# Layer 1's gate and up products by seven block products, in two phases of 512 tokens

## The chip, the cores and the metric

The kernel runs on one core of a Trainium2 chip. The metric is the device time of one execution in microseconds (us). The core has TensorE (PE in the profile; its weight loads are listed as PEld), VectorE (DVE), ScalarE (ACT), GpSimd (POOL) and SyncE (SP), which issues most DMAs. The engines run their own instruction streams in order and meet at semaphores.

## The reference

A block of two layers works on 1024 latent tokens of width 1024, with 256 context tokens as a prefix. Layer 0 mixes Fourier groups with windowed attention, layer 1 is a two-dimensional neighbourhood attention on a grid of 16 rows by 64 columns. Each layer ends in a SwiGLU FFN of width 2816:

```
def _swiglu(h, wg, wu, wd):
    return (jax.nn.silu(h @ wg) * (h @ wu)) @ wd
...
        x = x + g1 * o
        h = _rms(x, norm2_g[i]) * (1.0 + sc2) + sh2
        x = x + g2 * _swiglu(h, ffn_w_gate[i], ffn_w_up[i], ffn_w_down[i])
```

In the last layer only the latent tokens are kept. The case concerns layer 1 from its output projection (o before `x + g1 * o`) to the end.

## The kernel before

Everything stands transposed: 128 channels on the partitions, tokens along the free axis. A width of 1024 is eight tiles (KT = 8), 2816 is 22 tiles (NF = 22). Each fp32 number is split in two fp32r parts, hi (a rounded copy) and lo (the rest), and each product of tiles is three matmuls, hi by hi, hi by lo, lo by hi (`mm3`, L72 to L76, the three PE lines of the profile). So weights and activations both have to be split: a CAST on ACT gives hi, a subtraction on DVE gives lo.

In layer 1, `Dense` (L740 on) does the output projection, the norm, and the FFN. `weights` (L769 to L777) loads a raw tile of 128x1024 on the SP queue into one of two raw slots, casts it on ACT (L775), subtracts on DVE (L776), into a ring of four hi/lo tiles. `out_proj` (L779) makes each of eight output tiles over 24 matmuls of 512 columns into PSUM (`d_ps`), and DVE adds it to the residual x (L793). It runs twice, for tokens 0 to 511 and 512 to 1023; beside the second run go the norm of the first half (`norm`, L799 to L834: squares on ACT, sums on POOL or DVE, then nrm_t, h_hi, h_lo).

`ffn` (L836) walks over the 22 f tiles. `gate_up` makes, for each f and each half of the tokens, gate (`g_ps`) and up (`u_ps`), 24 matmuls of 512 columns each, then Silu on ACT (L860), the product on DVE (L862) and its split (L863 on ACT, L864 on DVE). `down` takes a block of two or three f's, and makes for each half eight chunks `d_ps` of 6 or 9 matmuls, which DVE adds to x (L878). Both halves use the same split weights: a weight is loaded and split once. x is kept in row order, and attention's output is in the order of grid columns, so x is read and written through a rearranged view (`xs`, `by_col`). In the last block each finished tile of x leaves as one DMA of 512 KB on ACT's queue (L1225).

Attention before it (L1087 to L1211) has its order written out by hand; its last matmuls are `po` (L1168), whose splits (L1177) write the tiles h_hi and h_lo (L1071). Elsewhere in this stage, the build's scheduler sets each engine's order, from the order of the code and its own estimate of when operands are there, and each engine then keeps to it. A tile pool with n buffers lets a new tile wait until an old one's last reader is done.

## Time and profile before

| | us |
|---|---|
| median of 3 runs (lowest, highest) | 2942.49 (2939.51, 2943.05) |
| the profiled execution | 2940.7 |
| its span, first to last instruction | 2938.9 |
| PE busy in it | 2860.1 |
| DVE, ACT, POOL busy in it | 1381.5, 875.5, 313.6 |
| first `d_ps` of layer 1's output projection starts at | 2095.0 |

The page first gives busy times by engine, then 40 equal slices with the clock granted to TensorE, the DMA queues, the chain of work that ended last, the costliest groups of instructions, and the DMAs. Groups are written `line engine operation out<-in shape xcount | busy us, mean ns of one | idle of the engine before them, and what ended it`. A timeline row starts with the start and the duration in us, and `[3.23 <-PE ...]` behind it is the idle time before it and what ended that. A PE row's duration includes the pipeline, so the pace of matmuls is read from the distance of their starts.

### The profile page before, as it was taken

To read this page: it belongs to the slowest core of one execution; us is meant where nothing else is said; L and a number is where in the kernel's file an instruction comes from. 1 tells how busy PE (TensorE), PEld (TensorE's weight loads), DVE (VectorE), ACT (ScalarE), POOL (GpSimd) and SP (SyncE) were. 2 spreads that over 40 slices of the span, in tenths; PEclk is the share of its full clock that TensorE was granted. 3 is DMA by queue.
4 is the path that set the end of the run, shared out by engine and by line. 5 is a ranking of instruction groups with operands and counts; after the bars stand their busy time and mean duration, and the time that the engine had idled before them with its cause. 6 is when DMAs were issued, how large, how long until landed. Compare 5 with 4: busy or idle time off the path is not lost. (4 is left out here: it accounts for less than half of the span.)

```text
span 2938.9 us, 38168 instructions
## 1 busy us (share of the span) xinstructions
PE 2860.1 (97%) x15290; PEld 2316.5 (79%) x15290; DVE 1381.5 (47%) x2530; ACT 875.5 (30%) x1672; POOL 313.6 (11%) x442
## 2 busy tenths in 40 slices
...
PEclk9989999999999999999999999999999999999999
...
GB/s 277 75 128 222 214 218 151 65 43 36 29 51 29 44 29 44 44 36 37 44 81 149 107 109 153 180 180 161 130 79 44 50 51 43 43 51 51 43 48 67
DMA packets 117218, 267.20 MB, mean 91 GB/s; under 512 B 9232, under 2 KB 67088, under 8 KB 110000
## 3 DMA queue, kind: packets, MB, share of 16 engines
...
## 5 line engine op out<-in xcount | busy, mean ns | idle before, releaser
L775 ACT CAST w_hi<-w_raw 128x1024 fp32r<-128x1024 f32 x188 | 195.3, 1049 | 881.3 <-PE d_ps L75 488.4
L878 DVE SCALAR_TENSOR_TENSOR x<-d_ps,mod,x 128x512 f32<-128x512 f32 (+1 forms) x400 | 348.1, 880 | 166.4 <-PE d_ps L76 165.9
L776 DVE TENSOR_TENSOR w_lo<-w_raw,w_hi 128x1024 fp32r<-128x1024 f32 x184 | 224.2, 1226 | 287.9 <-ACT w_hi L775 283.3
L862 DVE TENSOR_TENSOR sg<-sg,u_ps 128x512 f32<-128x512 f32 (+1 forms) x110 | 69.8, 634 | 570.5 <-PE u_ps L76 570.5
L74 PE MATMUL d_ps<-act_hi,w_hi 128*128 128x512 f32 (+1 forms) x880 | 328.0, 373 | 3.4 <-DVE x L878 3.4
L75 PE MATMUL d_ps<-act_lo,w_hi 128*128 128x512 f32 (+1 forms) x880 | 327.9, 373 | 1.3 <-DVE act_lo L864 1.3
L76 PE MATMUL d_ps<-act_hi,w_lo 128*128 128x512 f32 (+1 forms) x880 | 328.0, 373 | 0.0
L74 PEld LDWEIGHTS d_ps<-act_hi,w_hi 128*128 128x128 f32 x880 | 165.7, 188 | 37.4 <-DVE x L878 5.6
L75 PEld LDWEIGHTS d_ps<-act_lo,w_hi 128*128 128x128 f32 x880 | 165.7, 188 | 32.5 <-DVE act_lo L864 1.7
L76 PEld LDWEIGHTS d_ps<-act_hi,w_lo 128*128 128x128 f32 x880 | 165.7, 188 | 31.2
L75 PE MATMUL u_ps<-o_lo,w_hi 128*128 128x512 f32 (+1 forms) x528 | 188.6, 357 | 0.0
L76 PE MATMUL u_ps<-o_hi,w_lo 128*128 128x512 f32 (+1 forms) x528 | 188.6, 357 | 0.0
L74 PE MATMUL u_ps<-o_hi,w_hi 128*128 128x512 f32 (+1 forms) x528 | 188.6, 357 | 0.0
L76 PE MATMUL g_ps<-o_hi,w_lo 128*128 128x512 f32 (+1 forms) x528 | 188.5, 357 | 0.0
L75 PE MATMUL g_ps<-o_lo,w_hi 128*128 128x512 f32 (+1 forms) x528 | 188.5, 357 | 0.0
L74 PE MATMUL g_ps<-o_hi,w_hi 128*128 128x512 f32 (+1 forms) x528 | 188.5, 357 | 0.0
L580 POOL TENSOR_SCALAR pr<-pr,st 128x640 f32<-128x640 f32 (+2 forms) x208 | 156.0, 751 | 266.6 <-DVE st L579 176.0
L574 ACT ACTIVATE pr<-sm,st 128x640 f32<-128x640 f32 (+4 forms) x208 | 162.7, 782 | 31.1 <-POOL sm L563 22.3
L810 POOL TENSOR_TENSOR nrm_ss<-nrm_ss,nrm_sq 128x512 f32<-128x512 f32 (+1 forms) x38 | 48.4, 1274 | 1058.5 <-PE d_ps L76 935.6
L863 ACT CAST act_hi<-sg 128x512 fp32r<-128x512 f32 (+1 forms) x110 | 63.6, 578 | 298.3 <-DVE sg L862 298.3
L589 PE MATMUL pt_ps<-ident,pr 128*128 128x128 f32 x944 | 139.0, 279 | 5.8 <-ACT pt L593 2.8
L75 PE MATMUL g_ps<-h_lo,w_hi 128*128 128x512 f32 x352 | 139.6, 397 | 1.0 <-DVE h_lo L829 1.0
...
## 6 DMA issues: line engine op xcount, KB each, us to landing
...
w_raw<-w_gate SPq DMA_DIRECT2D x44, 512.0 KB, 3.2
w_raw<-w_up SPq DMA_DIRECT2D x44, 512.0 KB, 3.2
w_raw<-w_down SPq DMA_DIRECT2D x44, 512.0 KB, 3.2
...
w_raw<-w_out SPq DMA_DIRECT2D x32, 512.0 KB, 3.3
w_raw<-w_in SPq DMA_DIRECT2D x24, 512.0 KB, 4.4
q<-q_d SPq DMA_DIRECT2D x14, 512.0 KB, 16.8
```

The costliest lines, as they stand in the source:

```text
L74: TE.matmul(out, lh, rh, start=first, stop=False)
L75: TE.matmul(out, lh, rl, start=False, stop=False)
L76: TE.matmul(out, ll, rh, start=False, stop=last)
L574: S.activation(self.pr[:, :n], self.sm[:, :n], AF.Exp, bias=st[:, 0:1], scale=-1.0, accum_out=st[:, 1:2])
L580: G.tensor_scalar(self.pr[:, :n], self.pr[:, :n], st[:, 3:4], 0.0, ALU.mult, ALU.add)
L589: TE.transpose(pt[:, b * P:(b + 1) * P], self.pr[:, (b0 + b) * P:(b0 + b + 1) * P], ident)
L775: S.copy(hi, raw)
L776: eng.tensor_tensor(lo, raw, fl(hi), ALU.subtract)
L810: adder(i).tensor_tensor(ss, ss, sq, ALU.add)
L862: V.tensor_tensor(sg[:, :n], sg[:, :n], u_ps[:, :n], ALU.mult)
L863: S.copy(a_hi[:, sl], sg[:, :n])
L878: V.scalar_tensor_tensor(xs, self.shaped(ps[:, :n]), vec(l, 5)[:, dt, v:v + 1], xs, ALU.mult, ALU.add)
```

## The change

For one f, gate and up together are a product of a 2x2 block matrix of weights with a 2x2 block matrix of activations: the two halves of the 1024 input channels (k = 0 to 3, and 4 to 7) by gate and up, and two halves of 256 tokens. The new code computes it with seven block products instead of eight, by a scheme of Strassen's kind. It needs four sums of activation blocks (`combine`, made once per phase on POOL, then split by ACT and DVE to `c_hi`, `c_lo`) and four differences of weight blocks per f (`t1` to `t4`, on POOL). `gate_up1` has for each f and phase 7 products of 4 tiles by 3 matmuls of 256 columns, ACT casts of the seven weight blocks of 128x512, the lo parts of five on DVE and of two (b21, b22) on POOL, and additions of the products on DVE out of PSUM. The FFN runs once for tokens 0 to 511 and once for 512 to 1023, so each raw weight is loaded and split twice.

The output projection is also rewritten in two phases (`out_proj1`): x is now kept in grid-column order, the old residual is loaded again for each tile (`x_old`), and weights are split in halves of 128x512 into a ring of six. Raw weights, `x_old`, the block sums `s_sum` and later `h_in` share four slots of 128x1024. The normalized activations of the second phase are kept in DRAM (`h_d`) and loaded at the phase boundary. The down weights are split into the room of the attention output (`w_room`, named h1_hi and h1_lo in the rows below), two sets used in turn. The output leaves in eight DMAs of 256 KB per phase in column order, and the host's rearrangement of the result follows it.

```diff
-    bg, bg_cm = pools.open("big1", side="right")
-    h_hi = bg.tile([P, KT, SEQ], F32R, name="h_hi")
-    h_lo = bg.tile([P, KT, SEQ], F32R, name="h_lo")
+
+    h_out, bg_cms = [None, None], [None, None]
+    for i in (1, 0):
+        bg, bg_cms[i] = pools.open(f"big1{i}", side="right")
+        h_out[i] = [bg.tile([P, KT, 512], F32R, name=f"h{i}_{n}") for n in ("hi", "lo")]
...
-            hi, lo = (h[:, pr, g * 256:(g + 1) * 256] for h in (h_hi, h_lo))
+            hi, lo = (h[:, pr, g % 2 * 256:(g % 2 + 1) * 256] for h in h_out[g // 2])
...
-    dl = Dense(1, SEQ, (C0, C1), h_hi, h_lo, x, by_col=True)
-    own = norm2(C0)
-    dl.out_proj(io["w_out1"], (C0,), lambda dt: nc.sync.dma_start(x[:, dt], x_d[:, dt]), (own,))
-    last = norm2(C1, lambda i: V)
-    dl.out_proj(io["w_out1"], (C1,), None, (last,), own)
...
+    wr, wr_cm = pools.open("raw1", bufs=4)
+    ww, ww_cm = pools.open("ring1", bufs=6)
+    wk, wk_cm = pools.open("wk1")
+    pd, pd_cm = pools.open("pd1", bufs=2, psum=True)
+    pm, pm_cm = pools.open("pm1", bufs=1, psum=True)
+    pp, pp_cm = pools.open("pp1", bufs=5, psum=True)
+    HT = 256
+
+    def raw_weights(src):
+        raw = wr.tile([P, KT, P], F32, name="w_raw")
+        nc.sync.dma_start(raw, src)
+        return raw
+
+    def parts_of(src, eng=V):
+
+        hi, lo = (ww.tile([P, 4, P], F32R, name=n) for n in ("w_hi", "w_lo"))
+        S.copy(hi, src)
+        eng.tensor_tensor(lo, src, fl(hi), ALU.subtract)
+        return hi, lo
+
+    def out_proj1(ci, own, side=iter(())):
+        h_hi, h_lo = h_out[ci]
+        for dt in reversed(range(KT)):
+            raw = raw_weights(io["w_out1"][dt])
+            ws = [parts_of(raw[:, i:i + 4]) for i in (0, 4)]
+            old = wr.tile([P, SEQ], F32, name="x_old", tag="w_raw")
+            nc.sync.dma_start(old, x_d[:, dt])
+            ps = pd.tile([P, 512], F32, name="d_ps")
+            for k in range(KT):
+                hi, lo = ws[k // 4]
+                mm3(ps, hi[:, k % 4], lo[:, k % 4], h_hi[:, k], h_lo[:, k], k == 0, k == KT - 1)
+            cols = slice(ci * 32, ci * 32 + 32)
+            V.scalar_tensor_tensor(x[:, dt, ci * 512:ci * 512 + 512].rearrange("p (c r) -> p c r", r=GH),
+                                   ps.rearrange("p (c r) -> p c r", r=GH), vec(1, 2)[:, dt, 0:1],
+                                   old.rearrange("p (r c) -> p c r", c=GW)[:, cols], ALU.mult, ALU.add)
+            advance(own, 1)
+            advance(side, 3)
...
+    def norm1s(ci, adder, done):
...
+            both = []
+            for k in (i, i + 4):
+                t = wk.tile([P, 512], F32, name="nrm_t", tag="t", bufs=4)
+                V.scalar_tensor_tensor(t, x[:, k, ts], nA[3][:, k, 0:1], r, ALU.mult, ALU.mult)
+                h = wk.tile([P, 512], F32, name="nrm_h", bufs=2)
+                S.activation(h, t, AF.Identity, bias=vec(1, 3)[:, k, 0:1], scale=1.0)
+                both.append(h)
+                yield
+            done(i, *both)
...
+    def combine(i, h0, h4):
+        s = wr.tile([P, 4, HT], F32, name="s_sum", tag="w_raw")
+        G.tensor_tensor(s[:, 0], h0[:, M2], h4[:, M2], ALU.add)
+        G.tensor_tensor(s[:, 1], s[:, 0], h0[:, M1], ALU.subtract)
+        G.tensor_tensor(s[:, 2], h0[:, M1], h0[:, M2], ALU.subtract)
+        G.tensor_tensor(s[:, 3], h4[:, M1], s[:, 1], ALU.subtract)
+        for sl, src in ((slice(0, 1), h0[:, M1].unsqueeze(1)),
+                        (slice(1, 3), h4.rearrange("p (a n) -> p a n", a=2)), (slice(3, 7), s)):
+            S.copy(c_hi[:, sl, i], src)
+            V.tensor_tensor(c_lo[:, sl, i], src, fl(c_hi[:, sl, i]), ALU.subtract)
+
+    def product7(w, slot):
+        ps = pp.tile([P, 512], F32, name="p_ps")[:, 0:HT]
+        for k in range(4):
+            mm3(ps, w[0][:, k], w[1][:, k], c_hi[:, slot, k], c_lo[:, slot, k], k == 0, k == 3)
+        return ps
...
+    def gate_up1(f, side=iter(())):
+        g, u = raw_weights(io["w_gate"][1, f]), raw_weights(io["w_up"][1, f])
+        b11, b21, b12, b22 = g[:, 0:4], g[:, 4:8], u[:, 0:4], u[:, 4:8]
+        t1, t2, t3, t4 = (wk.tile([P, 4, P], F32, name=n, tag="t", bufs=4) for n in ("t1", "t2", "t3", "t4"))
+        p1, u2, u3, sg = (wk.tile([P, HT], F32, name=n) for n in ("p1", "u2", "u3", "sg"))
+        av = wk.tile([P, 2, HT], F32, name="av", bufs=2)
+        hi, lo = (wk.tile([P, 512], F32R, name=n, bufs=4) for n in ("act_hi", "act_lo"))
+        w = parts_of(b11)
+        G.tensor_tensor(t1, b12, b11, ALU.subtract)
+        G.tensor_tensor(t2, b22, t1, ALU.subtract)
+        ps = product7(w, 0)
+        S.copy(p1, ps)
+        w = parts_of(t2)
+        G.tensor_tensor(t3, b22, b12, ALU.subtract)
+        ps = product7(w, 4)
+        V.tensor_tensor(u2, ps, p1, ALU.add)
+        w = parts_of(t3)
+        G.tensor_tensor(t4, t2, b21, ALU.subtract)
+        ps = product7(w, 5)
+        V.tensor_tensor(u3, ps, u2, ALU.add)
+        w = parts_of(t1)
+        ps = product7(w, 3)
+        V.tensor_tensor(av[:, 1], ps, u3, ALU.add)
+        V.tensor_tensor(u2, ps, u2, ALU.add)
+        w = parts_of(t4)
+        ps = product7(w, 2)
+        V.tensor_tensor(u3, u3, ps, ALU.subtract)
+        S.activation(u3, u3, AF.Silu)
+        w = parts_of(b21, G)
+        ps = product7(w, 1)
+        V.tensor_tensor(av[:, 1], av[:, 1], u3, ALU.mult)
+        V.tensor_tensor(sg, ps, p1, ALU.add)
+        S.activation(sg, sg, AF.Silu)
+        w = parts_of(b22, G)
+        ps = product7(w, 6)
+        V.tensor_tensor(u2, ps, u2, ALU.add)
+        V.tensor_tensor(av[:, 0], u2, sg, ALU.mult)
+        avf = av.rearrange("p a n -> p (a n)")
+        S.copy(hi, avf)
+        V.tensor_tensor(lo, avf, fl(hi), ALU.subtract)
+        advance(side, 6)
+        return hi, lo
...
+    w_room = [t.rearrange("p k n -> p (k n)").rearrange("p (f h t k n) -> p f h t k n", f=2, h=2, t=2, n=P)
+              for t in h_out[1]]
...
+    def down1(ci, fs, acts, last):
+        w_in = w_room[fs[0] // 2 % 2]
+        ts = slice(ci * 512, ci * 512 + 512)
+        raws = [raw_weights(io["w_down"][1, f]) for f in fs]
+        for h in range(2):
+            for i, raw in enumerate(raws):
+                src = raw[:, 4 * h:4 * h + 4]
+                S.copy(w_in[:, i, h, 0], src)
+                V.tensor_tensor(w_in[:, i, h, 1], src, fl(w_in[:, i, h, 0]), ALU.subtract)
+            for dt in range(4 * h, 4 * h + 4):
+                ps = pd.tile([P, 512], F32, name="d_ps")
+                for i in range(2):
+                    mm3(ps, w_in[:, i, h, 0, dt % 4], w_in[:, i, h, 1, dt % 4], *acts[i], i == 0, i == 1)
+                V.scalar_tensor_tensor(x[:, dt, ts], ps, vec(1, 5)[:, dt, 0:1], x[:, dt, ts], ALU.mult, ALU.add)
+                if last:
+                    nc.scalar.dma_start(io["out"][:, dt, ts], x[:, dt, ts])
...
+    own0 = norm1s(0, G, combine)
+    out_proj1(0, own0)
...
+    own1 = norm1s(1, V, keep)
+    out_proj1(1, own1, own0)
+    advance(own0, 99)
+    for ci in range(2):
+        acts = {}
+        for f in range(NF):
+            acts[f] = gate_up1(f, own1)
+            if f % 2 == 0 and 2 <= f < NF - 2:
+                down1(ci, (f - 2, f - 1), [acts.pop(f - 2), acts.pop(f - 1)], False)
+        for f in (NF - 4, NF - 2):
+            down1(ci, (f, f + 1), [acts.pop(f), acts.pop(f + 1)], f == NF - 2)
+            if f == NF - 4 and ci == 0:
+                for i in range(4):
+                    h = wr.tile([P, 2, 512], F32, name="h_in", tag="w_raw")
+                    for n in range(2):
+                        nc.sync.dma_start(h[:, n], h_d[:, i + 4 * n])
+                    combine(i, h[:, 0], h[:, 1])
...
-    return np.ascontiguousarray(o.transpose(2, 1, 0).reshape(1, SEQ, D))
+
+    o = o.reshape(P, KT, GW, GH).transpose(3, 2, 1, 0)
+    return np.ascontiguousarray(o.reshape(1, SEQ, D))
```

Three places of the order. Rows are: line, operation, output<-inputs, shape; the number behind a name tells tiles apart.

First, DVE at the start of the second output projection. Before (x(18372) and x(18423) are the adds of its first and second tile, w_lo 18464 and 18499 the weights of its third and fourth):

```order
L776 TENSOR_TENSOR w_lo_18464<-w_raw_18461,w_hi_18463 128x1024
L793 SCALAR_TENSOR_TENSOR x_18001<-d_ps_18313,mod1_72,x_18001 128x32x16
L776 TENSOR_TENSOR w_lo_18499<-w_raw_18496,w_hi_18498 128x1024
L82 TENSOR_TENSOR nrm_v_18344<-nrm_v_18344 128x4
L83 SCALAR_TENSOR_TENSOR nrm_v_18344<-nrm_v_18344 128x4
L84 SCALAR_TENSOR_TENSOR nrm_v_18344<-nrm_v_18344 128x4
L827 SCALAR_TENSOR_TENSOR nrm_t_18357<-x_18001,nA3_76,nrm_r_18355 128x512
L827 SCALAR_TENSOR_TENSOR nrm_t_18360<-x_18001,nA3_76,nrm_r_18355 128x512
L827 SCALAR_TENSOR_TENSOR nrm_t_18398<-x_18001,nA3_76,nrm_r_18355 128x512
L829 SCALAR_TENSOR_TENSOR h_lo_14612<-nrm_t_18357,mod1_72,h_hi_14611 128x512
L793 SCALAR_TENSOR_TENSOR x_18001<-d_ps_18372,mod1_72,x_18001 128x32x16
```

After (x(18433) and x(18493) are the adds of the second and third tile, w_lo 18484 and 18488 the two halves of the third tile's weights):

```order
L1254 SCALAR_TENSOR_TENSOR x_18006<-d_ps_18433,mod1_72,x_old_18431 128x512
L1279 SCALAR_TENSOR_TENSOR nrm_t_18462<-x_18006,nA3_76,nrm_r_18415 128x512
L1271 TENSOR_TENSOR nrm_ss_18397<-nrm_ss_18397,nrm_sq_18459 128x512
L1279 SCALAR_TENSOR_TENSOR nrm_t_18477<-x_18006,nA3_76,nrm_r_18415 128x512
L1300 TENSOR_TENSOR c_lo_18358<-nrm_h_18464,c_hi_18357 128x2x256
L1300 TENSOR_TENSOR c_lo_18358<-s_sum_18466,c_hi_18357 128x4x256
L1300 TENSOR_TENSOR c_lo_18358<-nrm_h_18479,c_hi_18357 128x256
L1239 TENSOR_TENSOR w_lo_18484<-w_raw_18481,w_hi_18483 128x512
L1239 TENSOR_TENSOR w_lo_18488<-w_raw_18481,w_hi_18487 128x512
L1254 SCALAR_TENSOR_TENSOR x_18006<-d_ps_18493,mod1_72,x_old_18491 128x512
```

Before, the splits of the third and fourth tile's weights stand ahead of the first tile's add; now the third tile's stand behind the second's add and behind a step of norm and combine. The pattern repeats for the next three tiles.

Second, POOL in the loop over f, where it had no instruction. Here 20130 and 20132 are gate and up of the first f of a pair, 20282 and 20284 of its second, 20510 and 20512, 20662 and 20664 those of the next pair:

```order
L1239 TENSOR_TENSOR w_lo_20262<-w_raw_20132,w_hi_20261 128x512
L1316 TENSOR_TENSOR t1_20514<-w_raw_20512,w_raw_20510 128x512
L1317 TENSOR_TENSOR t2_20515<-w_raw_20512,t1_20514 128x512
L1321 TENSOR_TENSOR t3_20516<-w_raw_20512 128x512
L1325 TENSOR_TENSOR t4_20517<-t2_20515,w_raw_20510 128x512
L1239 TENSOR_TENSOR w_lo_20394<-w_raw_20282,w_hi_20393 128x512
L1239 TENSOR_TENSOR w_lo_20414<-w_raw_20284,w_hi_20413 128x512
L1316 TENSOR_TENSOR t1_20666<-w_raw_20664,w_raw_20662 128x512
L1317 TENSOR_TENSOR t2_20667<-w_raw_20664,t1_20666 128x512
L1321 TENSOR_TENSOR t3_20668<-w_raw_20664 128x512
L1325 TENSOR_TENSOR t4_20669<-t2_20667,w_raw_20662 128x512
L1239 TENSOR_TENSOR w_lo_20622<-w_raw_20510,w_hi_20621 128x512
```

Twelve operations make a period. In raw slots, 20512 takes the place of 20132, 20664 that of 20284, and both down tiles of the next stage (20814, then 20816) that of 20510, one after the other.

Third, DVE in the down stage of that pair. Before, at the end of a down stage:

```order
L878 SCALAR_TENSOR_TENSOR x_18001<-d_ps_21866,mod1_72,x_18001 128x32x16
L878 SCALAR_TENSOR_TENSOR x_18001<-d_ps_21874,mod1_72,x_18001 128x32x16
L776 TENSOR_TENSOR w_lo_22009<-w_raw_22006,w_hi_22008 128x1024
L776 TENSOR_TENSOR w_lo_22015<-w_raw_22012,w_hi_22014 128x1024
L862 TENSOR_TENSOR sg_21922<-sg_21922,u_ps_21897 128x512
L864 TENSOR_TENSOR act_lo_21895<-sg_21922,act_hi_21894 128x512
```

After (d_ps 20442 to 20502 are the eight chunks, 20814 the first down weight of the next pair):

```order
L1369 SCALAR_TENSOR_TENSOR x_18006<-d_ps_20442,mod1_72,x_18006 128x512
L1347 TENSOR_TENSOR act_lo_20296<-av_20294,act_hi_20295 128x512
L1369 SCALAR_TENSOR_TENSOR x_18006<-d_ps_20450,mod1_72,x_18006 128x512
L1369 SCALAR_TENSOR_TENSOR x_18006<-d_ps_20458,mod1_72,x_18006 128x512
L1364 TENSOR_TENSOR h1_hi_14611<-w_raw_20814,h1_hi_14611 128x512
L1369 SCALAR_TENSOR_TENSOR x_18006<-d_ps_20466,mod1_72,x_18006 128x512
L1364 TENSOR_TENSOR h1_hi_14611<-w_raw_20814,h1_hi_14611 128x512
L1369 SCALAR_TENSOR_TENSOR x_18006<-d_ps_20478,mod1_72,x_18006 128x512
```

Before, splits follow a stage's adds; now the split of the next pair's first down weight stands between the third and the fourth add of this pair, and PSUM has two buffers for these chunks (`pd`), not three.

33 lines of the change are left out of this document (25 added, 8 removed).

## The prediction

> **What bounds the kernel now.** I read the page first (busy time, slices, chain), then windows over layer 1, then its groups by form.
>
> ```profile
> span 2938.9 us, 38168 instructions
> ...
> PE 2860.1 (97%) x15290; PEld 2316.5 (79%) x15290; DVE 1381.5 (47%) x2530; ACT 875.5 (30%) x1672; POOL 313.6 (11%) x442
> ...
> PEclk9989999999999999999999999999999999999999
> ...
> PE 34%; DVE 1%; ACT 1%; issue 0%; ACTq 0%; DVEq 0%
> ```
>
> TensorE is busy for 97% of the span at nearly full clock, and the chain names little but PE lines. The changed stage is visible in these windows (columns: length; busy time and count of PE, PEld, DVE, ACT, POOL; clock, DMA share, GB/s):
>
> ```profile
> 2190.00:2300.00 110.00, 107.36 (x464) 85.46 (x464) 53.78 (x58) 28.64 (x38) 0.00 (x0) 1.00 0.11 39
> 2300.00:2939.00 639.00, 633.76 (x2720) 510.86 (x2718) 285.76 (x274) 99.65 (x130) 0.00 (x0) 1.00 0.15 51
> 2400.00:2900.00 500.00, 500.00 (x2146) 402.94 (x2145) 225.94 (x217) 81.57 (x106) 0.00 (x0) 1.00 0.14 47
> ```
>
> In layer 1's FFN, PE never waits: 500.00 us for 2146 matmuls of 512 columns is 0.2330 us each. DVE is idle for more than half of the stage, and POOL does nothing. Fewer PE cycles therefore turn into time only as long as the other engines keep up.
>
> **What the products save.** A 256-column matmul with its own weight load starts every 0.1177 us: 48 of them in layer 0 lie between these two rows, 5.53 us apart in 47 steps.
>
> ```profile
> 830.52 0.28 PE L74 MATMUL g_ps<-o_hi,w_hi 128*128 128x256 f32 x1
> ...
> 836.05 0.28 PE L76 MATMUL u_ps<-o_hi,w_lo 128*128 128x256 f32 x1
> ```
>
> Per f, gate and up cost 96 x 0.2330 = 22.37 us now, and 2 phases x 7 products x 12 matmuls = 168 x 0.1177 = 19.77 us after. 22 f's give **-57.1 us**. The down products keep their 96 matmuls per f. So the gain is 2.6 us per f, and any wait above that in a stage that had none turns it around.
>
> **The price on the other engines.** These rows carry the durations (mean ns of one):
>
> ```profile
> L810 POOL TENSOR_TENSOR nrm_ss<-nrm_ss,nrm_sq 128x512 f32<-128x512 f32 x24 | 33.5, 1396 | 113.8 <-ACT nrm_sq L809 113.6
> L1117 POOL TENSOR_TENSOR btab<-btab,mask 128x256 f32<-128x256 f32 x32 | 23.4, 731 | 8.9 <-DMA btab<-rel_bias 8.9
> L406 POOL TENSOR_TENSOR qs<-rb,qs 128x512 fp32r<-128x512 f32 x10 | 15.5, 1552 | 97.3 <-ACT qs L405 97.3
> L864 DVE TENSOR_TENSOR act_lo<-sg,act_hi 128x512 fp32r<-128x512 f32 x44 | 30.3, 688 | 16.1 <-ACT act_hi L863 16.1
> L793 DVE SCALAR_TENSOR_TENSOR x<-d_ps,mod,x 128x512 f32<-128x512 f32 x11 | 13.3, 1213 | 14.8 <-PE d_ps L76 14.8
> L775 ACT CAST w_hi<-w_raw 128x1024 fp32r<-128x1024 f32 x73 | 75.7, 1049 | 393.4 <-PE d_ps L75 215.4 <-PE g_ps L75 81.2 <-PE u_ps L75 50.9
> L863 ACT CAST act_hi<-sg 128x512 fp32r<-128x512 f32 x44 | 27.3, 620 | 120.9 <-DVE sg L862 120.9
> L828 ACT ACTIVATE h_hi<-nrm_t,mod 128x512 fp32r<-128x512 f32 x16 | 11.6, 723 | 13.8 <-DVE nrm_t L827 13.8
> ...
> w_raw<-w_gate SPq DMA_DIRECT2D x44, 512.0 KB, 3.2
> ```
>
> By their sums alone the engines have room: per pair of f's (30.96 us of PE: two gate_ups of 9.89 and 48 down matmuls of 0.2330, 11.18) POOL has 12 operations, 12 x 1.40 = 16.8 us. What counts is the ring. There are four raw slots for gate, up and both down tiles of a pair, the slots come free only when POOL has split b21 and b22, and POOL's order alternates splits and differences. The POOL and DVE orders shown above give one closed chain per pair (X, Y the two f's of a pair, p one POOL operation of 128x512):
>
> - product 1 of X, 12 x 0.1177 = 1.41, frees the weight slot that b22 of X needs; its cast 0.62 (the act_hi row) with a hand-off of about 0.2; POOL's split of it, p.
> - That frees the slot for up of the next X: load 3.35 (3.2 to landing, and the issue).
> - POOL: four differences of the next X, then both splits of Y, 6p. Load of the next Y's up, 3.35.
> - POOL: four differences of the next Y, then the split of the next X's b21, 5p. Its slot C takes the first down tile of the next pair: load 3.35.
> - Cast 0.62 and split 0.69 of that down tile (L1363, L1364). On DVE that split stands **ahead of this pair's fourth x add**, and with two PSUM banks for down, chunks 6 to 8 wait for this add: 0.73, a hand-off of 0.2, and 3 x 6 x 0.2330 = 4.19 of matmuls. Then the next pair's product 1 follows on PE.
>
> The sum is 18.7 + 12p per pair, against 30.96 on PE alone. It decides from p = 1.02 us on. The x add's 0.73 is layer 0's row without the column order, which the new layout resembles:
>
> ```profile
> 1500.08 0.73 DVE L878 SCALAR_TENSOR_TENSOR x<-d_ps,mod,x 128x512 f32<-128x512 f32 x1
> ...
> 1504.09 2.05 DVE L829 SCALAR_TENSOR_TENSOR o_lo<-nrm_t,mod,o_hi 128x512 fp32r<-128x512 f32 x1
> 1506.07 0.73 DVE L878 SCALAR_TENSOR_TENSOR x<-d_ps,mod,x 128x512 f32<-128x512 f32 x1
> 1506.72 1.16 DVE L827 SCALAR_TENSOR_TENSOR nrm_t<-x,nA,nrm_r 128x512 f32<-128x512 f32 x1
> 1507.81 1.11 DVE L829 SCALAR_TENSOR_TENSOR o_lo<-nrm_t,mod,o_hi 128x512 fp32r<-128x512 f32 x1
> ```
>
> ```profile
> 1501.01 4.30 POOL L810 TENSOR_TENSOR nrm_ss<-nrm_ss,nrm_sq 128x512 f32<-128x512 f32 x2 [10.28 <-ACT nrm_sq L809]
> 1506.07 1.27 POOL L810 TENSOR_TENSOR nrm_ss<-nrm_ss,nrm_sq 128x512 f32<-128x512 f32 x1 [0.76 <-ACT nrm_sq L809]
> ```
>
> The POOL rows give p from both sides: 1.27 for one that begins beside DVE's PSUM add, 2.15 each for the two at 1501.01 beside DVE splits with two SBUF inputs (one of these splits took 2.05 instead of 1.11), and 1.55 in the mean for L406, which also writes fp32r. I take the mean of the 24 of the same shape, 1.40: 18.7 + 16.8 = 35.5 us per pair, **4.5 us of wait**. There are 7 such pairs in the first phase and 8 in the second, 15 x 4.5 = **+68 us**; p = 1.27 gives 15 x 3.0 = 45, p = 1.55 gives 15 x 6.3 = 95.
>
> The Trainium skill, page "GPSIMD Engine Reference", section "Key points", says that POOL shares its SBUF interfaces with VectorE, contending with DVE instructions that have two SBUF inputs, and speaks so against putting this arithmetic on POOL beside DVE's splits. The rows at 1501.01 and 1504.09 agree; no row here shows which share of the new operations will meet. Taken in full, the rule gives the third rival below.
>
> **The second out-projection phase** is the other large term. The norm and the block sums of the first 512 tokens now run beside it, and DVE's order puts the weight split of the third output tile behind the x add of the second and a whole step of combine. Before, weights are kept four tiles ahead and norm arithmetic does not hold PE up:
>
> ```profile
> 2149.10 1.23 DVE L776 TENSOR_TENSOR w_lo<-w_raw,w_hi 128x1024 fp32r<-128x1024 f32 x1
> ...
> 2153.39 3.26 DVE L827 SCALAR_TENSOR_TENSOR nrm_t<-x,nA,nrm_r 128x512 f32<-128x512 f32 x3 [2.01 <-ACT nrm_r L172]
> ...
> 2157.23 1.20 DVE L793 SCALAR_TENSOR_TENSOR x<-d_ps,mod,x 128x512 f32<-128x512 f32 x1
> ...
> 2171.65 1.21 DVE L776 TENSOR_TENSOR w_lo<-w_raw,w_hi 128x1024 fp32r<-128x1024 f32 x1
> ```
>
> In the new order one tile takes: x add 1.2, norm product 0.73, ACT's shift 0.72, three POOL operations of 128x256 2.2 (the 731 row), ACT's cast of the four sums 1.05, of the second half 0.35 (half of 0.62, rounded up), of the weights 0.62, DVE's split 0.69, some seven hand-offs 1.2: 8.8 us, then the 22 matmuls behind the split with a hand-off, 5.3. That is 14.1 us instead of 24 x 0.2330 = 5.6, so +8.5 for three tiles, and about +7 for the fourth, whose step of combine has one norm product less: **+32 us**. Bounds: 20, if half of the chain slides under the matmuls, and 40 with POOL slowed as above.
>
> **Smaller terms.** Attention to out-projection, +2.5: now the first d_ps matmuls fill PE while the last po waits (rows below, nine of them, 2.3 us), and in the new order they stand after it, with the first load's slot lying over attention's last q.
>
> ```profile
> 2093.77 1.30 PE L1168 MATMUL po<-pt,v 128*64 128x256 f32 x12
> 2095.00 0.50 PE L74 MATMUL d_ps<-h_hi,w_hi 128*128 128x512 f32 x1
> ...
> 2097.30 2.17 PE L1168 MATMUL po<-pt,v 128*64 128x256 f32 x20
> ```
>
> First gate_ups of phase one, +5 (2 to 8): ACT copies p1 ahead of the cast for product 2, so product 2 waits for copy 0.35, cast 0.62, split 0.69 and hand-offs, 1.9 us, and the next two for their four POOL differences. First pair of each phase +2 in all: its loads find no lead. Phase boundary, +6 (0 to 12): POOL has 16 block sums of 0.73, 11.7 us, besides its 12 operations, and PE has only the last down stage of 11.18 to cover them; loads of the stored h pass through the same slots. At the end the output leaves in eight writes of half the size and the last x add is 0.5 shorter, -0.5. The 22 phase-two weight loads and splits done again cost nothing by their sums: they are in the chain above.
>
> Sum against the profiled execution, 2940.7 us (span 2938.9; the median of the runs, 2942.5, is 1.8 above it): 2940.7 - 57.1 + 68 + 32 + 2.5 + 5 + 2 + 6 - 0.5 = 2998.6. **Forecast 2998 us, slower by 1.9%.**
>
> **Rivals.**
>
> *The waits are hidden, faster.* If the chain is looser than I read it (loads land earlier, or the down split finds the fourth x add already done), the loop runs at 30.96 per pair. For it: the engine sums leave DVE, ACT and POOL half idle. Against it: it needs p below 1.02, and no POOL row of 128x512 is under 1.27, or a slot free without its POOL split. With out_proj's 32 and the small terms it gives 2940.7 - 57.1 + 32 + 15 = 2931; with out_proj hidden too, 2899; all hidden, 2884. Chance 0.17.
>
> *The gain is cancelled.* p near 1.27, half of out_proj's wait: 2940.7 - 57.1 + 45 + 16 + 5 = 2950, and with a little less, no change. Chance of a result within 0.2% (5.9 us, about what a measurement of this kernel can tell from no change): 0.06.
>
> *POOL beside DVE is much slower.* If half of a pair's 12 POOL operations take the 2.15 of the row at 1501.01, the chain is 18.7 + 6 x 1.27 + 6 x 2.15 = 39.2, the wait 8.3 and the sum 15 x 8.3 = 124: 2998.6 + 56 = 3055. DVE's two-input operations fill about a third of a pair, so a full half is unlikely: 0.09.
>
> *PE doesn't get faster.* Each matmul loads its weights again, and if the loads set the pace, 256 columns would save nothing. The 48 rows at 0.1177 speak against it; a mean of 0.133 would already take the whole gain (22.37 / 168), giving 2998.6 + 57 = 3056. Chance 0.02.
>
> **How the numbers follow.** My case, both waits with p between 1.27 and 1.55, has 0.66 and its own range of 2962 to 3035 (45 and 20, with the small terms low, to 95 and 40). Faster by more than 0.2% has 0.17 (rival one and the fast end of the second), no change 0.06, slower 0.77 (my case, the two slow rivals, and what of the second stays above). The range takes in rival one without its hidden out-projection, and stops short of the two slow rivals: 2930 to 3045.
>
> **What would show it.** Right: in the FFN, PE rows in each down stage with an idle of about 4.5 us after the fifth chunk, released by DVE x (L1369), in turn behind L1364 and the down load; per pair about 35.5 us; POOL's t rows at 1.3 to 1.5; p_ps matmuls every 0.118 us. In the second out-projection, four tiles 14 us apart, PE waiting for DVE w_lo (L1239). Wrong: pairs 31 us apart; PE idle at the products instead of down (then the weight ring, not the down tile, is late); POOL rows at 1.0 or under. If the loop's wait is there but out_proj's isn't, the time is near 2967.

## The result, and the profile after

The changed kernel takes **3116.81 us** (median of four runs, 3114.27 to 3118.68), the kernel before 2941.71 on the same chips: a ratio of 1.0595, 95% interval 1.0577 to 1.0614. It is slower, as forecast, but by 175 us and not by 56, and outside the range.

The page of the changed kernel, and windows over layer 1 (columns as in the prediction; the last two windows answer to 2190 to 2300 and 2400 to 2900 of before):

```profile
span 3115.5 us, 43813 instructions
...
PE 2861.5 (92%) x16874; PEld 2375.9 (76%) x16874; DVE 1662.2 (53%) x3164; ACT 1062.6 (34%) x2127; POOL 723.7 (23%) x738
...
PEclk9989999999999999999999999999888989999989
...
PE 19%; POOL 6%; DMA 4%; DVE 4%; issue 4%; ACT 2%; POOLq 0%; ACTq 0%; DVEq 0%
```

```profile
2160.00:2200.00 40.00, 16.80 (x49) 11.69 (x48) 18.87 (x24) 14.73 (x24) 10.99 (x12) 0.70 0.16 52
...
2190.00:2300.00 110.00, 84.21 (x466) 71.56 (x465) 73.81 (x101) 45.38 (x82) 48.03 (x35) 0.88 0.33 111
...
2400.00:2900.00 500.00, 408.41 (x2625) 361.10 (x2624) 346.03 (x525) 174.33 (x328) 228.73 (x165) 0.91 0.27 87
```

In the last of these windows PE was busy for 500 of 500 us and is now busy for 408; POOL, DMA and DVE now have 6, 4 and 4% of the chain that ended last; and the granted clock, 1.00 in this stage before, is 0.91, in the out-projection 0.70. PE's longest sums of waits from 2090 us on (total, times, longest):

```profile
PE d_ps L74 <- DVE x L1369: 129.4, 30, 8.5
PE d_ps L74 <- ACT w_hi L1238: 30.9, 5, 7.7
```

These are the two waits that the prediction named, at the places it named: the down stage's x add, and the out-projection's weights. What it did not name is seen behind each of them. PE's rows after one of the waits (start, duration):

```profile
2454.12 0.79 PE L74 MATMUL d_ps<-act_hi,h_hi 128*128 128x512 f32 x1 [6.66 <-DVE x L1369]
2454.71 0.63 PE L75 MATMUL d_ps<-act_lo,h_hi 128*128 128x512 f32 x1
2455.13 0.63 PE L76 MATMUL d_ps<-act_hi,h_hi 128*128 128x512 f32 x1
2455.56 0.63 PE L74 MATMUL d_ps<-act_hi,h_hi 128*128 128x512 f32 x1
...
2458.97 0.46 PE L76 MATMUL d_ps<-act_hi,h_hi 128*128 128x512 f32 x1
2459.27 0.39 PE L74 MATMUL d_ps<-act_hi,h_hi 128*128 128x512 f32 x1
2459.51 0.40 PE L75 MATMUL d_ps<-act_lo,h_hi 128*128 128x512 f32 x1
```

The matmuls of 512 columns start 0.427 us apart for 4.8 us after the wait, and 0.233 apart from then on; against the usual pace that is 2.3 us lost. The clock granted to TensorE shows the same directly, in windows just before, in and just after this slow stretch (columns as above, the clock is the third number from the end):

```profile
2445.00:2452.20 7.20, 2.45 (x11) 1.66 (x9) 0.00 (x0) 0.14 (x1) 3.53 (x3) 1.00 0.24 73
2452.30:2459.10 6.80, 4.98 (x12) 3.92 (x13) 3.37 (x5) 1.81 (x4) 0.00 (x0) 0.50 0.29 77
2459.15:2466.00 6.85, 6.85 (x55) 6.54 (x54) 4.69 (x8) 2.32 (x5) 1.29 (x1) 1.00 0.31 86
```

The clock falls to one half during the wait, 1.8 us before it ends, and returns 5.0 us after.

The account, over all of PE's rows from 2090 us to the end: 177.9 us of idle time (3.3 us before the change), and 75 us by which matmuls start later than their usual pace without any idle time. Against these stand the products, which are faster than predicted; 105 matmuls of 256 columns lie between these two rows, 0.1133 us each (0.1137 is the mean of 3652):

```profile
2420.02 0.28 PE L74 MATMUL p_ps<-c_hi,w_hi 128*128 128x256 f32 x1
...
2431.92 0.28 PE L74 MATMUL p_ps<-c_hi,w_hi 128*128 128x256 f32 x1
```

Over 3696 matmuls that is 14.8 us more than the 57.1 of the prediction. 177.9 - 3.3 + 75 - 71.9 = 177.7, where the two profiled executions differ by 3117.3 - 2940.7 = 176.6.

| stage (us of the span) | idle | slow clock | predicted for both |
|---|---|---|---|
| attention's end and out-projection (2090 to 2235) | 32.4 | 12.4 | 34.5 |
| first gate_ups and first pair (to 2296) | 10.8 | 7.7 | 6 |
| loop, both phases (2296 to 2584, 2738 to 3024) | 110.3 | 40.8 | 68 |
| phase boundary and second start (2584 to 2738) | 20.7 | 12.2 | 7 |
| end | 3.7 | 2.2 | -0.5 |

In the fourth row, 8.0 us of the idle time are the first x-add wait of phase two, which the prediction counted among its 15 pairs.

### One pair of the loop, link by link

The prediction's closed chain can be followed in the rows. POOL, then SP's issues, then DVE:

```profile
2421.87 1.29 POOL L1239 TENSOR_TENSOR w_lo<-w_raw,w_hi 128x512 fp32r<-128x512 f32 x1 [14.38 <-ACT w_hi L1238]
2428.19 1.29 POOL L1316 TENSOR_TENSOR t<-w_raw 128x512 f32<-128x512 f32 x1 [5.03 <-DVE w_lo L1239]
...
2434.29 3.45 POOL L1239 TENSOR_TENSOR w_lo<-w_raw,w_hi 128x512 fp32r<-128x512 f32 x2
2441.85 1.28 POOL L1316 TENSOR_TENSOR t<-w_raw 128x512 f32<-128x512 f32 x1 [4.11 <-DMA w_raw<-w_up]
...
2447.26 1.27 POOL L1239 TENSOR_TENSOR w_lo<-w_raw,w_hi 128x512 fp32r<-128x512 f32 x1
2462.88 1.29 POOL L1239 TENSOR_TENSOR w_lo<-w_raw,w_hi 128x512 fp32r<-128x512 f32 x1 [14.35 <-ACT w_hi L1238]
```

```profile
2421.85 0.33 SPq L1232 DMA_DIRECT2D w_raw<-w_gate  x1
2423.19 0.33 SPq L1232 DMA_DIRECT2D w_raw<-w_up  x1
...
2437.76 0.33 SPq L1232 DMA_DIRECT2D w_raw<-w_up  x1
2448.55 6.46 SPq L1232 DMA_DIRECT2D w_raw<-w_down  x2
```

```profile
2427.28 0.69 DVE L1239 TENSOR_TENSOR w_lo<-t,w_hi 128x512 fp32r<-128x512 f32 x1 [0.17 <-ACT w_hi L1238]
...
2452.71 0.69 DVE L1364 TENSOR_TENSOR h_lo<-w_raw,h_lo 128x512 fp32r<-128x512 f32 x1 [7.71 <-ACT h_lo L1363]
2453.32 0.74 DVE L1369 SCALAR_TENSOR_TENSOR x<-d_ps,mod,x 128x512 f32<-128x512 f32 x1
```

From one split of b22 to the next it is 2462.88 - 2421.87 = 41.0 us, and each link can be set against the prediction:

| link | measured | predicted |
|---|---|---|
| POOL's split, next up loaded, first difference starts | 6.32 | 4.75 |
| six POOL operations | 9.57 | 8.40 |
| load of the next up | 4.09 | 3.35 |
| five POOL operations | 6.70 | 7.00 |
| load of the down tile, its cast and split, the fourth x add, PE starts | 5.57 | 5.59 |
| three chunks of matmuls | 6.55 | 4.19 |
| product 1, cast of b22 | 2.21 | 2.23 |
| sum | 41.0 | 35.5 |

Of the 5.5 us by which the pair is longer, 2.36 are the slow clock inside the chain, 1.57 and 0.74 are the two loads of up, and 0.87 is POOL in both its links together. The row at 2428.19 names DVE's split of 2427.28 as what released POOL, but the load landed at 2427.97 as well, 4.78 us after its issue at 2423.19. In all 32 waits over 3 us of POOL for a first difference, from 2300 us on and whichever releaser the row names, it starts 0.13 to 0.22 us after up has landed: the load decides. Up is issued 1.3 to 1.7 us behind gate, while gate's load is still under way, and takes longer than gate and down. Issue to landing, median, from 2296 to 2584 us, where all three had 3.2 before the change:

```profile
w_raw<-w_down SPq DMA_DIRECT2D x15, 512.0 KB, 3.5
w_raw<-w_gate SPq DMA_DIRECT2D x14, 512.0 KB, 3.5
w_raw<-w_up SPq DMA_DIRECT2D x14, 512.0 KB, 4.5
```

That the two loads slow each other was not tried in a run.

### The profile page after: what moved, and what is told of

The parts are those of the page before. It is cut to its first block, busy times and chain, and to the rows that moved or that the text cites. A ratio compares the mean times of both kernels' runs of the same rounds, so it can differ in the third digit from the quotient of the medians.

```text
span 3115.5 us, 43813 instructions
## 1 busy us (share of the span) xinstructions
PE 2861.5 (92%) x16874; PEld 2375.9 (76%) x16874; DVE 1662.2 (53%) x3164; ACT 1062.6 (34%) x2127; POOL 723.7 (23%) x738
## 5 line engine op out<-in xcount | busy, mean ns | idle before, releaser
L74 PE MATMUL p_ps<-c_hi,w_hi 128*128 128x256 f32 x1232 | 343.8, 279 | 10.3 <-ACT p L1319 5.6
L76 PE MATMUL p_ps<-c_hi,w_lo 128*128 128x256 f32 x1232 | 344.7, 280 | 5.2 <-DVE w_lo L1239 4.0
L75 PE MATMUL p_ps<-c_lo,w_hi 128*128 128x256 f32 x1232 | 342.5, 278 | 0.0
L74 PEld LDWEIGHTS p_ps<-c_hi,w_hi 128*128 128x128 f32 x1232 | 233.5, 190 | 13.2 <-ACT p L1319 6.2
L76 PEld LDWEIGHTS p_ps<-c_hi,w_lo 128*128 128x128 f32 x1232 | 232.9, 189 | 9.9 <-DVE w_lo L1239 6.6
L75 PEld LDWEIGHTS p_ps<-c_lo,w_hi 128*128 128x128 f32 x1232 | 233.4, 189 | 1.0
L878 DVE SCALAR_TENSOR_TENSOR x<-d_ps,mod,x 128x512 f32<-128x512 f32 (+1 forms) x240 | 157.5, 661 | 125.4 <-PE d_ps L76 125.4
L74 PE MATMUL d_ps<-act_hi,w_hi 128*128 128x512 f32 (+1 forms) x528 | 189.4, 359 | 3.4 <-DVE x L878 3.4
L75 PE MATMUL d_ps<-act_lo,w_hi 128*128 128x512 f32 (+1 forms) x528 | 189.3, 358 | 1.3 <-DVE act_lo L864 1.3
L76 PE MATMUL d_ps<-act_hi,w_lo 128*128 128x512 f32 (+1 forms) x528 | 189.3, 359 | 0.0
```

The costliest lines, as they stand in the source:

```text
L74: TE.matmul(out, lh, rh, start=first, stop=False)
L75: TE.matmul(out, lh, rl, start=False, stop=False)
L76: TE.matmul(out, ll, rh, start=False, stop=last)
L878: V.scalar_tensor_tensor(xs, self.shaped(ps[:, :n]), vec(l, 5)[:, dt, v:v + 1], xs, ALU.mult, ALU.add)
```

## The experiments

The letters of the theories are explained in the expectations. All times stand against 3116.8 us for the changed kernel and about 2940 for the one before; in parentheses stand the ratio to the kernel before and its 95% interval. "The pair" is the time from one pair of f's to the next in the loop.

### Keeping TensorE busy: e1

Into the fifth chunk of 14 of the down stages go 24 matmuls with zero weights, 78 us of added PE work (14 x 24 x 0.233); DVE's order of the stage is held.

```
+ for z in range(24): TE.matmul(ps, zr, acts[0][0], start=False, stop=z == 23)
```

> The changed kernel with 24 more matmuls of 512 columns (5.6 us at full clock) with a zero weight tile, added to the fifth chunk of the 14 down stages from f = 2 to 15 of each phase, DVE's order left as it is. They stand where PE waits about 7.3 us for DVE's fourth x add, so they lengthen no wait. Theory A (the slow matmuls behind each wait, 0.427 us instead of 0.233, are TensorE's clock halved after the idle): PE idles under 2 us there, the clock stays at 1.0, the chunks behind the wait run at 0.233 and each of these pairs is about 1.7 us shorter: 3117 - 14 x 1.7 = 3093, faster with 79 us of work added. Theory B (they are slow for another reason, as reads that collide with loads): the slow rows stay, and the time is 3117 or more.

3103.75 us (1.0556, 1.0538 to 1.0574): 13 us *faster* with 78 us more work. The wait at the x add falls from 129.4 to 60.4 us, the time lost at slow clock from 75 to 57. The added matmuls lie in time that PE waited anyway, and a shorter wait costs less clock. The gain is about half of theory A's 24 us: in these stages waits of 1.0 to 3.3 us are left (9.3 in the first), and most of those over 2 us still cost clock. With the windows above, the slow clock is a cost of its own and comes from the waits.

### The links of the chain: e2, e5, e15, e16

e2 holds the split of the next pair's first down tile behind the last x add.

```
+ with contextlib.ExitStack() as st:
+     for ins in adds[-1:]: st.enter_context(tc.issue_after(ins))
      V.tensor_tensor(w_in[:, i, h, 1], src, fl(w_in[:, i, h, 0]), ALU.subtract)
```

> The changed kernel with one difference: DVE's split of a pair's down weights is queued behind the last x add of the pair before it, and not ahead of its fourth. Raw slots, POOL work and products are as they were. Theory A (the loop's wait is that order: the fourth x add behind a split that waits for a load): the wait of about 7.3 us in some 15 down stages and the 1.7 us of slow clock behind it go, pairs are 31 to 32 us, the time is 3117 - 15 x 9 = 2980. Theory B (the ring of four raw slots and POOL's 12 operations bound the pair, whatever DVE's order): the wait moves to the products or to the next down weights, pairs stay above 36 us, the time above 3045.

3106.96 us (1.0564, 1.0548 to 1.058): 10 us less, far from what theory A gave and in the range of theory B. The pair is 39 us. But the edit changed more than one link: the build's scheduler also moved POOL's differences of the next f behind both splits of Y. DVE's rows of this kernel show what holds the x adds now:

```profile
2432.53 1.12 DVE L1240 TENSOR_TENSOR w_lo<-t,w_hi 128x512 fp32r<-128x512 f32 x1 [2.87 <-ACT w_hi L1239]
...
2438.72 1.42 DVE L1240 TENSOR_TENSOR w_lo<-t,w_hi 128x512 fp32r<-128x512 f32 x1
...
2441.74 0.74 DVE L1376 SCALAR_TENSOR_TENSOR x<-d_ps,mod,x 128x512 f32<-128x512 f32 x1
```

The first add of the stage stands behind the splits of the differences, which POOL delivers late. e5 gives the ring a fifth raw slot.

```
- wr, wr_cm = pools.open("raw1", bufs=4)
+ wr, wr_cm = pools.open("raw1", bufs=5)
```

> The changed kernel with five raw slots instead of four (4 KB more per partition, which is free); nothing else is edited, the scheduler sets its order again. Theory C (the period is the life of the raw slots: gate and up keep theirs until b21 and b22, the sixth and seventh of seven blocks, are split, and the next pair's loads and POOL differences only follow): a slot of their own for the down tiles takes one load and one split out of the chain, pairs fall from 41 to 33 to 36 us, the time to 3117 - 15 x 6 = 3027 or less. Theory D (POOL's and DVE's operations, slowed beside each other, are the bound): pairs stay at 39 or more, the time above 3090.

3091.2 us (1.0514, 1.0493 to 1.0535), pair about 38: again a link is gone, and little is won; the time is theory D's, the pair lies between the two theories. These two runs left it open whether the predicted chain sets the 41 us at all. The two runs that follow leave the order of the loop on DVE as it is. e15 computes t3 twice, so POOL has two more operations per pair; e16 takes a PSUM bank from the products for down.

```
  G.tensor_tensor(t3, b22, b12, ALU.subtract)
+ G.tensor_tensor(t3, b22, b12, ALU.subtract)
```

> The changed kernel with one more POOL instruction per f: the difference t3 is computed twice in a row. In the steady loop the order of POOL, DVE and PE is otherwise that of the changed kernel. Theory A: the closed chain of the prediction (split of b22, load, six POOL operations, load, five POOL operations, load of the down tile, its split ahead of the fourth x add, three chunks, product 1) sets the pair, and only its terms were mis-sized; then both new instructions of a pair lie in it, 2 x 1.45 us, so the pair goes from 41.0 to 43.9 us and the time, with 14 to 15 such pairs, to about 3117 + 42 = 3159 us. Theory B: another chain sets the pair and POOL has slack, as the later experiments with the order changed let one think; then the pair stays within 0.7 us of 41 and the time within 10 us of 3117.

```
- pd, pd_cm = pools.open("pd1", bufs=2, psum=True)
+ pd, pd_cm = pools.open("pd1", bufs=3, psum=True)
- pp, pp_cm = pools.open("pp1", bufs=5, psum=True)
+ pp, pp_cm = pools.open("pp1", bufs=4, psum=True)
```

> The changed kernel with three PSUM banks for down and four for the products, instead of two and five; DVE's order in the steady loop is unchanged, the split of the next down tile still stands ahead of the fourth x add. Theory A (closed chain through that x add): the sixth chunk no longer waits, two chunks instead of three follow the add, 12 matmuls at the half clock, 5.1 us, instead of the 6.55 us between the wait's end and product 1; the pair becomes 39.6 us and the time about 3117 - 14 x 1.45 = 3097 us, with the wait after the sixth chunk instead of the fifth. Theory B (the place of the wait is immaterial, another chain sets the pair): pair 41 and time 3117 within 6 us.

e15: 3179.41 us (1.0808, 1.0791 to 1.0826), the pair 44.2 us in the mean, so the whole of two POOL operations (expected 43.9). 13 to 14 pairs x 3.2 account for 45 of the 63 us; most of the rest is a wait that is new, 19.8 us of products for POOL's splits. e16: 3100.48 us (1.0538, 1.052 to 1.0555), the pair 39.8 (expected 39.6), with the wait one chunk later, directly behind the add that follows the split:

```profile
2449.47 0.69 DVE L1364 TENSOR_TENSOR h_lo<-w_raw,h_lo 128x512 fp32r<-128x512 f32 x1 [8.95 <-ACT h_lo L1363]
2450.09 0.74 DVE L1369 SCALAR_TENSOR_TENSOR x<-d_ps,mod,x 128x512 f32<-128x512 f32 x1
```

Lengthened by a known amount and shortened by a known amount, the pair follows both: the predicted chain does set the 41 us. Cutting it (e2, e5) uncovers others at 38 to 39 us, which hold the same operations of POOL and DVE.

### The out-projection: e4

Weights are split two tiles ahead, and the norm and block sums take two steps per tile, behind these splits.

```
+ queue = [split_w(KT - 1 - j) for j in range(2)]
  for dt in reversed(range(KT)):
+     if dt >= 2: queue.append(split_w(dt - 2))
+     ws = queue.pop(0)
...
-     advance(side, 3)
+     with tc.issue_after(cut[0]), tc.issue_after(cut[1]): advance(side, 2)
```

> The changed kernel with the second output projection's weights split two tiles ahead of their use, and two steps of the first half's norm and block sums after each tile instead of three. Theory A (PE waits there because the splits stand behind a step of norm and block sums): the four waits of about 7.6 us and the slow clock behind them, 12 us in all, go but for some 8 us: 3117 - 36 = 3081, PE waiting less than 10 us between 2100 and 2200. Theory B (norm and block sums fill ACT, POOL and DVE so far that their sum bounds the phase): less than 10 us gained, above 3107.

3085.63 us (1.0495, 1.0474 to 1.0516), 31 us less, near theory A's 3081. The 30.9 us of waits for w_hi fall to 1.0, and a new one stands at the end of the stage, where the last norm is left over:

```profile
PE d_ps L74 <- DVE x L1377: 129.1, 28, 9.6
PE pmisc L164 <- DVE nrm_ss L1279: 9.4, 1, 9.4
```

### Less work on POOL, or earlier: e3, e6, e7

e3 puts the splits of b21 and b22 on DVE. e6 makes their products second and third, so that their raw slots are read sooner (b22's product then stays in a PSUM bank). e7 is e6 with e4 and e5.

```
- w = parts_of(b21, G)      # e3: parts_of(b21); the same for b22
```

> The changed kernel with the two weight splits b21 and b22 on DVE, so that POOL has 8 operations in a pair instead of 12; nothing else is edited, though the scheduler now sets the down split behind the fourth x add and not the third. Theory A (POOL's 12 operations at 1.4 to 1.6 us are in the closed chain): four of them leave it, some 4 x 0.8 us net, and one chunk of 1.4 us is no longer behind the split: pairs 41 - 3.2 - 1.4 - 1.7 = about 35, the time 3117 - 15 x 6 = 3027. Theory B (DVE, which now has about 31 us of work in a pair at contended durations, becomes the bound): 3060 to 3117.

> The changed kernel with the seven products in another order, b21 and b22 as second and third (their sums taken later, the product of b22 waiting in its PSUM bank), still four raw slots, the same operations on every engine. Theory C: raw gate and up are free after the third split, some four products earlier (5.6 us and more), so the next loads and differences start that much earlier: pairs of 31 to 34 us, time 3117 - 15 x 8.5 = 2990. Theory D: the work on POOL and DVE is the same, pairs stay at 39 or more, the time above 3090.

> The reordered products, five raw slots, and the second output projection's weights split two tiles ahead with two steps of norm and block sums per tile. Theory C: nothing holds PE in the loop, pairs of 31.0 us; what is left is the start of the first phase (about 12), the output projection (about 8) and the phase boundary (about 10): 2940 - 57 + 30 = 2913, faster than before by 0.9%. Theory D: pairs above 36, the time above 2990.

e3: 3065.26 us (1.0426, 1.0397 to 1.0455), pair 36.5; e6: 3065.39 us (1.0426, 1.0405 to 1.0447), pair 37.4; e7: 3043.13 us (1.0355, 1.0337 to 1.0372). e3's time is in theory B's range, e6 lies between its two theories, and e7, forecast at 2913 if only the slots counted, is where theory D put it. e7 has neither the short ring nor the out-projection's wait, and its pair is still 37.5 us, with 88.3 us of waits for x adds. There DVE is idle for only 1.0 us between 2418.9 and 2439, the products' part of the pair, and its x adds stand at the end of that queue. The ring alone is refuted as the last bound.

### Taking work out: e8, e9

On e6 with e4: e8 leaves out DVE's five lo splits of gate and up (a constant zero tile in their place), e9 leaves out POOL's four differences (a constant zero tile is read instead). Both lack part of the arithmetic, so only their times are of use.

```
- w = parts_of(t2)          # e8, for b11, t1 to t4: hi_of(t2), lo = a zero tile
- G.tensor_tensor(t1, b12, b11, ALU.subtract)      # e9, t1 to t4
```

> The reordered products and the earlier splits of the output projection (four raw slots), with DVE's five weight splits of each gate_up left out: the lo part of these blocks is a constant tile of zeros, so the output is not the reference's; every matmul, cast and POOL operation is still there. DVE loses 10 operations of 0.68 to 0.96 us in a pair, pairs were 37.4 us with the reordered products. Theory E (DVE's work, lengthened beside POOL's, comes too late for the x adds): pairs fall to 31 to 32 us, the time to about 3035 - 15 x 6 = 2945. Theory F (POOL's chain of differences and splits and the loads between them bind, DVE only passes the delay on): pairs stay at 36 or more, the time at 3010 or more.

> The same kernel with DVE's splits in, and POOL's four weight differences of each gate_up left out: t1 to t4 are a constant tile of zeros, so the output is not the reference's; every matmul, cast and split is still there. POOL has 4 operations in a pair instead of 12. Theory E in its narrow form (DVE's own work is the bound, at 0.68 us a split it has 24 to 25 us in a pair, but badly placed): pairs stay above 35. Theory F: pairs fall to 31 to 32, the time to about 2945. If both this and the kernel without DVE's splits come down to 31, the bound is what the two engines share, and relief on either is enough.

2963.99 and 2943.85 us (one run each), pairs of 34.4 and 33.0. The nearest complete kernel is e7 with 3043 (it has a fifth slot besides). e9's time is the one of theory F, e8's lies between E and F. Groups from 2300 to 2900 us, of the changed kernel, of e9, of e8:

```profile
L1239 POOL TENSOR_TENSOR w_lo<-w_raw,w_hi 128x512 fp32r<-128x512 f32 x59 | 87.8, 1497 | 180.6 <-ACT w_hi L1238 180.6
...
L1239 DVE TENSOR_TENSOR w_lo<-t,w_hi 128x512 fp32r<-128x512 f32 x120 | 112.5, 939 | 12.7 <-ACT w_hi L1238 12.1
```

```profile
L1244 POOL TENSOR_TENSOR w_lo<-w_raw,w_hi 128x512 fp32r<-128x512 f32 x72 | 94.8, 1324 | 476.8 <-ACT w_hi L1244 475.8
...
L1244 DVE TENSOR_TENSOR w_lo<-flat,w_hi 128x512 fp32r<-128x512 f32 x144 | 100.8, 700 | 41.9 <-ACT w_hi L1244 41.3
```

```profile
L1341 POOL TENSOR_TENSOR t<-w_raw 128x512 f32<-128x512 f32 x36 | 46.7, 1298 | 9.9 <-DMA w_raw<-w_up 7.8
```

Without POOL's differences DVE's split takes 0.700 us and not 0.939; without DVE's splits POOL's differences take 1.30 to 1.37 and not 1.41 to 1.46. Each is slowed by the other, DVE by a third, POOL by about a tenth. Beside e6, whose order they have, DVE's splits fall in e9 from 1.00 to 0.70 us (of differences, eight a pair) and from 1.39 to 0.72 (of b11, two a pair), 3.7 us of the 4.4 by which the pair is shorter. But e9 also takes eight operations out of POOL's chain and e8 ten out of DVE's, so these two runs don't show what part of the gain is the sharing alone. The Trainium skill, page "GPSIMD Engine Reference", section "Key points", which the prediction weighed, says that the two share SBUF interfaces; these runs agree, and give its price here.

### Placing the work: e10 to e14

All five start from e7. e10 computes t1 and t3 on DVE, with three PSUM banks for down; e11 has b21's and b22's splits on DVE instead.

> A whole kernel: reordered products, five raw slots, earlier splits of the output projection, two of the four weight differences (t1, t3) on DVE instead of POOL, three PSUM banks for down and four for the products. POOL has 8 operations in a pair, DVE 4 more at 0.68. If DVE and POOL bound the pair by the sum of their two-input operations, which falls by 4 x (1.28 - 0.68) = 2.4 us, pairs of 34 to 35: 3043 - 15 x 3 = 2998. If POOL's chain binds, less: 2975. If DVE's own time binds: 3043 or more.

> As the mixed kernel, but all four differences on POOL and the splits of b21 and b22 on DVE instead. Same counts on both engines; in this one POOL is out of the chain that frees the raw slots. If the slots' release is what counts, it is faster than the mixed one, 2975 to 2990; if only the shared time counts, the same, about 2998.

2984.87 us (1.0149, 1.012 to 1.0179) and 2970.92 us (1.0102, 1.0073 to 1.0131); e11's pair is 34.0 us and its clock in the loop 1.00. What the third bank gives by itself here was not run (on the changed kernel it gave 16 us, e16). That e11 is the faster fits the release of the slots, from which it takes POOL's splits. DVE is now full through the products, with room in the down stage. e12 makes down stages of four f's, e13 puts half a down stage, four chunks, behind each gate_up; both are e11 otherwise, except that the second half's norm waits until f = 2 (and that e12 has a fifth pair of act tiles, with the norm's tiles in raw slots). e14 is e13 with b21's split back on POOL.

```
- if f % 2 == 0 and 2 <= f < NF - 2:        # e11
-     down1(ci, (f - 2, f - 1), [acts.pop(f - 2), acts.pop(f - 1)], False)
+ if 2 <= f < NF - 2:                       # e13
+     g = f // 2 * 2
+     if f == g: w_in = down_w((g - 2, g - 1))
+     down1(ci, w_in, range(4 * (f - g), 4 * (f - g) + 4), [acts[g - 2], acts[g - 1]], False)
```

> The kernel with the splits of b21 and b22 on DVE, and: down in blocks of four f's (two at f = 16, 17), so that DVE has half as many x adds, 3 us less in a pair; five act tiles; the norm outputs of the second out-projection in the raw slots; the second half's norm not finished before f = 2. Every operation of the scheme is there. If DVE's time, 30.2 us in a pair of 34.0, is what is left as the bound, it has 27.3 us now and pairs come to 31.0 to 31.5 (a block of two pairs to 62 to 63): 2971 - 15 x 2.8 - 8 = 2921, faster than before by 0.7%. If it is DVE's order around the down stage (waits of 1.5 us for the first x add and 1.7 us in the products), these stay once per block: 2971 - 15 x 1.5 - 8 = 2940, the same as before.

> The kernel with the splits of b21 and b22 on DVE (e11), and: the eight chunks of a down stage in two halves, four behind each gate_up, and the second half's norm held behind the second product stage on PE. The same operations on each engine. If the unevenness is what is left (DVE has 11 us in a gate_up of 9.9 and 8.6 us in a down stage of 11.2), pairs fall from 34.0 to 31.0 to 32.0 and PE's wait of 9.8 us at the norm goes: 2971 - 15 x 2.5 - 9 = 2925, faster than before by 0.5%. If DVE's sum at the durations it has beside POOL is the bound, pairs stay at 33.5 to 34: 2955.

> The same with the split of b21 back on POOL: DVE has 2 operations of 0.68 us less in a pair, POOL 2 of 1.28 more. If DVE's sum binds in e13, this is faster than e13 by about 15 x 1 = 15 us; if what the two engines share binds (two-input operations on either), it is the same or slower by up to 15 x 1.2 = 18; if the unevenness was all, the same within 5.

e12: 2982.3 us (1.014, 1.0123 to 1.0157); e13: **2929.54 us (0.9963, 0.9951 to 0.9976), 0.4% faster than the kernel before**; e14: 2953.53 us (1.0042, 1.0027 to 1.0057). The window from 2400 to 2520 us, of e12, e13 and e14, one fence each:

```profile
2400.00:2520.00 120.00, 110.95 (x738) 100.55 (x737) 94.65 (x143) 43.36 (x84) 36.52 (x27) 0.99 0.30 96
```

```profile
2400.00:2520.00 120.00, 116.03 (x834) 106.70 (x834) 107.59 (x174) 54.10 (x100) 38.27 (x30) 1.00 0.30 98
```

```profile
2400.00:2520.00 120.00, 114.43 (x798) 103.74 (x797) 103.86 (x162) 50.72 (x93) 48.76 (x38) 1.00 0.29 97
```

e13 is near the 2925 us of its first theory, unevenness. e12 missed both of its theories (2921 and 2940) and is slower than e11, although DVE makes half as many x adds in it. Blocks of four cost 53 us more than halves: with four f's the waits stand at the products (PE for DVE's u and sg, 50 us from 2250 to 2900). That DVE's uneven load over the stage is the reason fits both runs; the act tiles and raw slots, in which e12 differs too, were not tried alone. In e13 DVE is busy for 107.59 of 120 us, evenly, no wait in the loop is over 2.6 us, and the half pairs take 15.1 to 16.5 us. e14 takes work *off* DVE and is 24 us slower, more than the 18 it allowed for: DVE's splits of the down weights then take 0.81 us in the mean and not 0.70, while those of b11 (1.28 and 1.30) and of the differences (0.86 and 0.85) stay, and PE waits 31.1 and not 23.3 us for x adds. So DVE's sum is not what is left. Whether it is the time in which both engines work side by side, or the order of the loop, these runs don't separate. In e13 the largest single wait that is left is 9.0 us, PE for the first weights of phase one:

```profile
PE d_ps L74 <- DVE x L1381: 23.3, 22, 2.6
PE p_ps L74 <- ACT w_hi L1240: 9.0, 1, 9.0
```

It was not worked on.

## Why the prediction was right or wrong

**Right.** The direction, and why: a gain of 2.6 us per f is smaller than the wait that it brings in. *What the products save* was 57.1 predicted and 71.9 measured, as 256 columns take 0.1137 us and not layer 0's 0.1177. *The second out-projection phase*, +32, has 30.9 us of waits, four of them at 6.9 to 7.7, though released by ACT's cast of the weights (L1238) and not by DVE's split; tiles are 16 us apart and not 14 (two of them between these rows), and the slow clock behind these waits, 2.3 to 3.2 us each, covers the difference. e4 gave 31 us back. The *closed chain per pair* is right in every link, with the wait after the fifth chunk as said; e15 and e16 bear it out. p was 1.40 predicted and 1.41 to 1.50 measured. Two rivals fell: the waits are not hidden, and PE does get faster.

```profile
2167.83 0.80 PE L74 MATMUL d_ps<-h_hi,w_hi 128*128 128x512 f32 x1 [7.70 <-ACT w_hi L1238]
...
2200.05 0.79 PE L74 MATMUL d_ps<-h_hi,w_hi 128*128 128x512 f32 x1 [7.63 <-ACT w_hi L1238]
```

**Wrong, the size.** Two things:

- The term that was mis-sized is *18.7 + 12p = 35.5, 4.5 us of wait, 15 pairs, +68*. The pair is 41.0, so 5.5 more for each of 14 pairs, 77 us. Of the 5.5, its link "3 x 6 x 0.2330 = 4.19 of matmuls" carries 2.36 (6.55, the clock) and its two links "load 3.35" of up carry 2.31: the price was that of gate's loads in the kernel before (3.2 to landing), where up now takes 4.5. POOL's speed, on which the prediction's range was built, carries only 0.87. The rival with POOL much slower came nearer to the time, 39.2 per pair and 3055, but by a mechanism that isn't there.
- A whole cost is missing from the sum: **after a wait PE runs at half clock.** It is 75 us in all; some 33 of them (14 x 2.36) are inside the 77 above. The sum priced PE's time behind every wait at 0.2330 us per matmul, because before the change no wait of PE in this stage was over 1.0 us and its rows showed no other pace. Layer 0 of the same trace did show it, behind a wait of 2.12 us: from the first to the second of these rows there are seven steps of 0.44 us each, and the granted clock of the window from 1523.90 to 1527.20 is 0.50.

```profile
1523.71 0.70 PE L74 MATMUL u_ps<-w_hi,o_hi 128*128 128x512 f32 x1 [2.12 <-ACT o_hi L828]
...
1526.77 0.63 PE L76 MATMUL u_ps<-w_hi,o_lo 128*128 128x512 f32 x1
```

Together: the sum had 115 us for waits and small terms (68 + 32 + 2.5 + 5 + 2 + 6 - 0.5). Measured are 174.6 us more idle time than before and 75 of slow clock, less the 14.8 that the products gave on top: 119.8 more than the sum, where the forecast fell 118.7 short (2998.6 against 3117.3 for the profiled execution).

The phase boundary and the starts were 33 and 18.5 us, against 7 and 6: there too the waits came with slow clock (12.2 and 7.7). That the block sums hold the shared slots for longer than the 11.18 us of one down stage is a reading of the order; how the boundary's 20.7 us of idle time divide among slots, POOL and loads was not tried.
